# A hybrid three-mixer layer: bonus term and output gate of each token group moved from the group's own step into the next step

## The chip, the cores and the metric

The kernel runs on one core of one Trainium2 chip. The metric is the device time of one execution in microseconds (us). The kernel before took 2331.53 us, the median of three runs (2328.48 to 2334.17).

## The reference, cut to what matters

The kernel computes one layer of a token model: 1024 latent tokens and 256 context tokens, 1024 channels, one input projection, three parallel token mixers (a gated linear recurrence, an RWKV-7 mixer, an S5 state-space mixer), a gated sum with an output projection, and a SwiGLU network. The change touches the RWKV-7 mixer alone. Its width is 512, in 8 heads of 64 channels. Cut to the lines at stake (`d` is the direction):

```python
kk = heads(k * k_k); kk = kk * lax.rsqrt(jnp.sum(kk * kk, axis=-1, keepdims=True) + 1e-12)
for d in range(2):
    iclr = jax.nn.sigmoid(a0[d] + ad[:, :, d] @ a2[d])
    k_d = heads(k * (1.0 + (iclr - 1.0) * k_a))
    y_d, s_d = wkv7_scan(r_h, heads(decay), k_d, v_h, kk, heads(iclr), s0[d], d == 1)
    bonuses.append(jnp.sum(r_h * k_d * r_k, axis=-1, keepdims=True) * v_h)
y = ((y - mean) * lax.rsqrt(var + RWKV_GN_EPS)).reshape(b, l, wdt) * ln_w + ln_b
y = y + (bonuses[0] + bonuses[1]).reshape(b, l, wdt)
return y * (jax.nn.sigmoid(gd) @ g2), jnp.stack(fins)
```

The bonus term and the output gate `g = sigmoid(gd) @ g2` need nothing of the scan. The kernel prepares from them two arrays per latent token, `ln_w * g` and `(bonus + ln_b) * g`, and the scan's result is later multiplied by the first and added to the second.

## The kernel before, in words

The program is written with a framework that tracks which instruction reads and writes which tile. It puts the semaphores in by itself, and it orders the instructions of each engine by a planner: the planner runs the program against its own model of times, and among the instructions that it takes to be ready it picks the one that was written first. So the order in the source is a priority and not the order of issue. On the chip each engine then works its list off in that fixed order.

The RWKV stage prepares heads in four pairs (`p` = 0 to 3). Two heads of 64 channels fill the 128 partitions. For each pair, `rwkv_pair` (L727) loads small weights, projects and shifts the key, value and receptance, and then goes through ten groups of 128 tokens (`g` = 0 and 1 are context, 2 to 9 are latent) in a loop of eleven steps (L868). A step works on three groups at once:

- `pre(g+1)` (L765): loads two low-rank inputs (`wdt`, L768, on SyncE), eight matmuls (L774), a tanh (`swa`, L777), and on VectorE a rescale (L778) and two scans along time (`cum`, L780 and L781).
- `mid(g)` (L785): two exponentials on ScalarE (`pf`, `pi`, L797 and L798), products on GpSimd (`t`, L807 and L809; `pcend`, L799 and L800) and on VectorE (`kr`, L810 and L814; `kb`, L811 and L812). For a latent group it then forms the bonus and the gate: a sum `ks` on GpSimd (L818), a product `ks` on VectorE (L819), two matmuls into one PSUM bank (L821: the sum over a head's channels; L822: `g2`), two VectorE instructions (`vs`, L824; `glt`, L825), one on ScalarE (`glt`, L826) and one store by SyncE (`gld`, L827).
- `fill(seg_fill)` (L875): two, two, one or four pieces (by pair) of an independent projection for the branch gates (`zg`, L1333; matmuls at L1309, three to a piece).
- `post(g-1)` (L830): 32 small matmuls of `kb` with `kr` (L843), four transposes (L855), one masked copy on VectorE (`al`, L844), five copies on ScalarE (`aq`, L851; `kt`, L856), five stores by SyncE (L857, L865).

The projections of the head pair's own inputs are the matmuls at L1303, which the planner lets run among the steps. After the eleven steps, a triangular inverse per pair (L895) starts on VectorE (L901, L904, L905) and goes on as some 60 small products on GpSimd (pairs 0 to 2) or VectorE (pair 3 and the context's own inverse; `nt`, L909 and L911). The next pair's preparation starts beside it; the reciprocal `rn` (L748) belongs to that.

In pair 3 step 9 drains the filler, and step 10 starts the scan over 40 chunks (`rwkv_chain`, L920), which runs for the next several hundred us. Its first dependent step needs the context's inverse.

What the tiles allow: matmul results go through five PSUM banks of one tag (`aux`, L1857), used in turn by `pre`, `mid` and `post`. The tiles `ks` and `vs` have two buffers each, `glt` has one. A write into a tile waits until the readers of its older content in that buffer are done.

Of the kernel before, what the change touches and what calls it, by code (L numbers as in the profile page):

```python
# [9 lines left out]
F32 = mybir.dt.float32  # L10
F32R = mybir.dt.float32r
AF = mybir.ActivationFunctionType
ALU = mybir.AluOpType
# [3 lines left out]
P = 128  # L17
# [618 lines left out]
class RwkvMixin:  # L636
# [90 lines left out]
    def rwkv_pair(s, p, pool):  # L727
        nc = s.nc
        V, G, S = nc.vector, nc.gpsimd, nc.scalar
        segs = ((0, NCTX), (NCTX, 512), (NCTX + 512, 512))  # L730
        c1 = lambda key: s.pv(key)[:, p : p + 1]
# [5 lines left out]
        g2 = pool.tile([P, P], F32, name="g2", tag="g2")  # L737
        nc.sync.dma_start(g2, s.i["rwkv_g2"][0][:, cols])
        k = s.rk_next or s.shift(12 + p, True, pool, "zk", 2)
# [4 lines left out]
        for t0, n in segs:  # L744
            ps = s.aux()
# [5 lines left out]
        st = {}  # L751
# [33 lines left out]
        def mid(g):  # L785
            lat = g > 1
            sl = slice(P * g, P * g + P)
            gl0 = P * (g - 2)
# [24 lines left out]
            if lat:  # L813
                V.tensor_tensor(kr[:, :, :, 32:64], bc(st["r"]), pcur, op=ALU.mult)  # L814
                ks = pool.tile([P, P], F32, name="ks", tag="ks", bufs=2)
                vs = pool.tile([P, P], F32, name="vs", tag="vs", bufs=2)
                k2 = t2.rearrange("p d c t -> p d (c t)")
                G.tensor_tensor(ks, k2[:, 0], k2[:, 1], op=ALU.add)  # L818
                V.scalar_tensor_tensor(ks, st["r"][:, sl], c1("rk"), ks, op0=ALU.mult, op1=ALU.mult)  # L819
                ps = s.aux()  # L820
                nc.tensor.matmul(ps[:, 0:P], s.bones, ks, start=True, stop=True)  # L821
                nc.tensor.matmul(ps[:, P : 2 * P], g2, s.gdt[:, gl0 : gl0 + P], start=True, stop=True)  # L822
                glt = pool.tile([P, 2, P], F32, name="glt", tag="glt")
                V.tensor_tensor(vs, ps[:, 0:P], st["v"][:, sl], op=ALU.mult)  # L824
                V.scalar_tensor_tensor(glt[:, 1], vs, c1("lnb"), ps[:, P : 2 * P], op0=ALU.add, op1=ALU.mult)  # L825
                S.activation(glt[:, 0], ps[:, P : 2 * P], AF.Copy, scale=c1("lnw"))  # L826
                nc.sync.dma_start(s.gl_d.rearrange("a k c t -> c a k t")[:, p, :, gl0 : gl0 + P], glt)  # L827
            st[g] = [kb, kr]

        def post(g):  # L830
            lat = g > 1
# [36 lines left out]
        for g in range(11):  # L868
            if g < 9:
                pre(g + 1)  # L870
            if g < 10:
                mid(g)
            if g == RSEG:
                vr()
            s.fill(s.seg_fill)  # L875
            if g:
                post(g - 1)
            if p == 3 and g == 2:
                s.rwkv_ctx_inverse(pool)
            if p == 3 and g == CB:  # L880
                s.chain_begin()
            if p == 3 and g in CTX_AT:
                next(s.chain)
            if p < 3 and g == 7:
                s.rk_next = s.shift(13 + p, True, pool, "zk", 2)
# [1096 lines left out]
```

## Time and profile before

| what | value |
|---|---|
| median of the runs | 2331.53 us |
| the profiled execution's own time | 2331.55 us |
| its span, first to last instruction | 2329.8 us |
| granted TensorE clock over the span | 0.952 of full |
| TensorE matmul busy | 2102.5 us (90%) |
| VectorE busy | 1508.0 us (65%) |
| ScalarE busy | 904.2 us (39%) |
| GpSimd busy | 986.0 us (42%) |

In the rows, PE is TensorE (matmuls), PEld its weight loads, DVE is VectorE, ACT is ScalarE, POOL is GpSimd, SP is SyncE. L819 is line 819 of the kernel. Times count from the first instruction. An arrow with an engine behind a bracketed number says how long the engine stood idle and what ended it. One matmul of the program in 32-bit floats shows as two records. A clock of 0.50 means that TensorE was granted 1.2 GHz of its 2.4 GHz.

The latent groups of the four pairs run from 741 to 803 us, 837 to 911, 944 to 1013 and 1033 to 1120; between them lie the starts of the next pair.

### The profile page before, as it was taken

Reading aid. Unit: us, or ns where it says so; the run is one execution under the profiler, and the core shown is the slowest. Engines: PE = TensorE matmul, PEld = TensorE weight load, DVE = VectorE, ACT = ScalarE, POOL = GpSimd, SP = SyncE. Lnnn points to the kernel's source line nnn. Section 1 sums busy time; section 2 is a strip of 40 time slices with the busy share of each in tenths; the row PEclk is TensorE's granted clock in tenths of the full one; section 3 lists DMA queues with packets and bytes.
Section 4 is the critical chain, followed back from the end, with each engine's and each line's share of the span. In section 5 each row is a group of like instructions: output and inputs, shape, how many; then the busy total and the mean of one; then the engine's idle time right before and its main releaser. Section 6 shows DMA issues by size and latency. Waiting matters only on the chain.

```text
span 2329.8 us, 38390 instructions
## 1 busy us (share of the span) xinstructions
PE 2102.5 (90%) x14573; PEld 1675.7 (72%) x14573; DVE 1508.0 (65%) x2218; ACT 904.2 (39%) x1698; POOL 986.0 (42%) x1169
## 2 busy tenths in 40 slices
PE   5979988887899988898699999898999999989998
PEld 3868866665778877776467676676788888878886
DVE  5656698889566888899843366936855555543533
ACT  5313354423334645454533333416433323233431
POOL 3662389955323494856100122544644444300302
PEclk8989999998999999998699999998999999999999
DMA  6634322221663535445967777544222222274540
GB/s 254 168 110 115 90 66 83 82 84 64 143 174 89 161 111 140 125 136 142 246 181 173 171 191 183 167 158 136 81 77 86 77 86 77 68 276 151 165 149 36
DMA packets 360550, 307.26 MB, mean 132 GB/s; under 512 B 66023, under 2 KB 311982, under 8 KB 359342
## 3 DMA queue, kind: packets, MB, share of 16 engines
q1 hardware_dynamic: 356782, 293.27, 43.5%
q10 hardware_dynamic: 2880, 10.49, 1.2%
q8 instruction: 115, 1.88, 0.3%
q0 software_dynamic: 704, 1.05, 0.2%
q14 instruction: 69, 0.57, 0.1%
HBM read 219.03 MB, written 85.70 MB: 131 GB/s over the span
## 4 chain that ended last, share of the span: by engine, by line
PE 56%; DVE 19%; POOL 9%; DMA 7%; issue 5%; ACT 3%; SPq 1%; DVEq 0%; POOLq 0%; ACTq 0%
PE mm L1563 18%; PE mm L1718 10%; PE mm L1303 8%; PE mm L1309 7%; PE cg L1011 2%; PE cg L985 2%; PE cu L998 2%; DMA wm<-in_w_mod_dram 1%; DVE zl L1296 1%; PE cy L1026 1%; POOL s L214 1%; DVE s5ct L522 1%; PE aux L609 1%; DVE macc L1269 1%; DVE rn L748 1%
## 5 line engine op out<-in xcount | busy, mean ns | idle before, releaser
L1563 PE MATMUL mm<-q,wt 128*128 128x512 f32 x1584 | 376.6, 398 | 4.5 <-DVE q L1477 3.2
L1563 PEld LDWEIGHTS mm<-q,wt 128*128 128x128 f32 x1584 | 299.4, 189 | 77.5 <-DVE q L1477 3.6
L1718 PE MATMUL mm<-wk,hk 128*128 128x512 f32 x960 | 224.2, 396 | 0.0
L1303 PE MATMUL mm<-xh,wh 128*128 128x512 f32 (+1 forms) x576 | 214.4, 380 | 8.4 <-ACT ya L180 6.1
L1303 PE MATMUL mm<-xl,wh 128*128 128x512 f32 (+1 forms) x576 | 214.3, 379 | 1.2 <-DVE xl L1219 1.2
L1718 PEld LDWEIGHTS mm<-wk,hk 128*128 128x128 f32 x960 | 180.4, 188 | 43.6
L1309 PE MATMUL mm<-xh,zh 128*128 128x512 f32 x384 | 159.6, 416 | 10.0 <-ACT zge L1345 5.8
L1309 PE MATMUL mm<-xl,zh 128*128 128x512 f32 x384 | 159.5, 415 | 0.0
L1303 PE MATMUL mm<-xh,wl 128*128 128x512 f32 (+1 forms) x576 | 141.2, 383 | 8.8 <-DVE wl L1296 6.6
L1303 PEld LDWEIGHTS mm<-xh,wh 128*128 128x128 f32 x576 | 114.3, 199 | 28.6 <-ACT ya L180 6.9
L1671 DVE TENSOR_TENSOR wk<-wraw,wk 128x512 fp32r<-128x512 f32 x80 | 55.9, 707 | 111.3 <-ACT wk L1670 111.3
L1303 PEld LDWEIGHTS mm<-xl,wh 128*128 128x128 f32 x576 | 113.8, 197 | 19.4 <-DVE xl L1219 1.5
L1309 PE MATMUL mm<-byt,bwh 128*128 128x512 f32 x384 | 118.6, 428 | 7.9 <-ACT bwh L1295 2.9
L1303 PEld LDWEIGHTS mm<-xh,wl 128*128 128x128 f32 x576 | 102.9, 197 | 30.1 <-DVE wl L1296 8.2
L1309 PE MATMUL mm<-xh,zl 128*128 128x512 f32 x384 | 110.1, 423 | 15.3 <-DVE zl L1296 15.3
L1691 POOL TENSOR_TENSOR acc<-acc,ot 128x512 f32<-128x512 f32 x14 | 19.0, 1358 | 225.7 <-DVE ot L1689 225.2
L1015 DVE TENSOR_TENSOR x<-cg,pcend 64x256 f32<-64x256 f32 x152 | 63.9, 421 | 77.9 <-PE cg L1011 35.4
L1476 ACT ACTIVATE wt<-wT 128x512 fp32r<-128x512 f32 x88 | 55.1, 631 | 142.5 <-PE mm L1563 130.5
L1309 PEld LDWEIGHTS mm<-xh,zl 128*128 128x128 f32 x384 | 75.4, 202 | 35.2 <-DVE zl L1296 18.3
L1269 DVE SCALAR_TENSOR_TENSOR macc<-wm,cs,macc 128x256 f32<-128x256 f32 x112 | 84.6, 755 | 22.3 <-DMA wm<-in_w_mod_dram 19.8
L1477 DVE TENSOR_TENSOR wt<-wt 128x512 fp32r<-128x512 f32 x66 | 60.5, 918 | 59.4 <-ACT wt L1476 59.0
L1293 POOL CAST bwh<-bwr 128x512 fp32r<-128x512 f32 x16 | 10.0, 624 | 209.6 <-PE mm L1309 112.1
(421 smaller groups left out, 4865.3 us busy)
## 6 DMA issues: line engine op xcount, KB each, us to landing
wt<-in_w_ffn_in_dram SPq DMA_DIRECT2D x44, 512.0 KB
wraw<-in_w_ffn_out_dram SPq DMA_DIRECT2D x44, 512.0 KB
wm<-in_w_mod_dram SPq DMA_DIRECT2D x64, 256.0 KB
gyl<-gyl SPq DMA_DIRECT2D x32, 512.0 KB
wr<-in_w_in_dram SPq DMA_DIRECT2D x27, 512.0 KB
zr<-in_w_in_dram SPq DMA_DIRECT2D x24, 512.0 KB
sgd<-zge SPq DMA_DIRECT2D x48, 256.0 KB
bsg<-sgd SPq DMA_DIRECT2D x48, 256.0 KB
```

Source lines behind the costliest of these rows:

```text
L985: s.pe = nc.tensor.matmul(ps[32 * q : 32 * q + 32, 64 * p : 64 * p + 64], gy[:, 2 * p + par, c - cb, 0:32], st["x"][:, p, par, :], start=T ...
L998: s.pe = nc.tensor.matmul(ps[o : o + 32, 64 * p : 64 * p + 64], st["tt"][32 * q : 32 * q + 32, p, st["cc"], :], st["gs"][32 * q : 32 * q + ...
L1011: s.pe = nc.tensor.matmul(sn[64 * par : 64 * par + 64, 64 * p : 64 * p + 64], sd[:, st["cc"], 2 * p + par, :], st["x"][:, p, par, :], star ...
L1015: V.tensor_tensor(xn[0:64, :, par, :], sn[r].rearrange("p (a k) -> p a k", a=4), vb(s.pcend[r, d, :, st["c"]], 64), op=ALU.mult)
L1269: nc.vector.scalar_tensor_tensor(acc, wm[:, j], s.cs[:, k + j, 0:1], acc, op0=ALU.mult, op1=ALU.add)
L1303: s.nc.tensor.matmul(ps, w(k), a(k), start=n == 0, stop=n == len(seq) - 1)
L1309: s.nc.tensor.matmul(ps, w[:, k], a[:, k], start=n == 0, stop=n == len(seq) - 1)
L1476: s.nc.scalar.activation(hi, raw, AF.Copy)
L1477: (eng or s.nc.vector).tensor_tensor(lo, raw, hi, op=ALU.subtract)
L1563: nc.tensor.matmul(ps, w[:, k], a[:, k], start=n == 0, stop=n == len(seq) - 1)
L1671: V.tensor_tensor(hl[:, 1], raw, hl[:, 0], op=ALU.subtract)
L1718: nc.tensor.matmul(banks[t, n], a[:, tk], b, start=k == 0 and q == 0, stop=k == NF - 1 and q == 2)
```

## The change: what it does

The part of `mid(g)` that begins with the two matmuls becomes a function of its own, `gate(g)`. The sum and the product that make `ks` stay in `mid(g)`; the tile is kept until the gate is formed. In the loop, `gate(g-1)` is written behind `post(g-1)`, so the gate of group `g` moves from the middle of step `g` to the end of step `g+1`. The instructions themselves, their shapes and buffers are as before.

```diff
             if lat:
                 V.tensor_tensor(kr[:, :, :, 32:64], bc(st["r"]), pcur, op=ALU.mult)
                 ks = pool.tile([P, P], F32, name="ks", tag="ks", bufs=2)
-                vs = pool.tile([P, P], F32, name="vs", tag="vs", bufs=2)
                 k2 = t2.rearrange("p d c t -> p d (c t)")
                 G.tensor_tensor(ks, k2[:, 0], k2[:, 1], op=ALU.add)
                 V.scalar_tensor_tensor(ks, st["r"][:, sl], c1("rk"), ks, op0=ALU.mult, op1=ALU.mult)
-                ps = s.aux()
-                nc.tensor.matmul(ps[:, 0:P], s.bones, ks, start=True, stop=True)
-                nc.tensor.matmul(ps[:, P : 2 * P], g2, s.gdt[:, gl0 : gl0 + P], start=True, stop=True)
-                glt = pool.tile([P, 2, P], F32, name="glt", tag="glt")
-                V.tensor_tensor(vs, ps[:, 0:P], st["v"][:, sl], op=ALU.mult)
-                V.scalar_tensor_tensor(glt[:, 1], vs, c1("lnb"), ps[:, P : 2 * P], op0=ALU.add, op1=ALU.mult)
-                S.activation(glt[:, 0], ps[:, P : 2 * P], AF.Copy, scale=c1("lnw"))
-                nc.sync.dma_start(s.gl_d.rearrange("a k c t -> c a k t")[:, p, :, gl0 : gl0 + P], glt)
+                st["ks", g] = ks
             st[g] = [kb, kr]
+
+        def gate(g):
+
+            sl = slice(P * g, P * g + P)
+            gl0 = P * (g - 2)
+            ks = st.pop(("ks", g))
+            vs = pool.tile([P, P], F32, name="vs", tag="vs", bufs=2)
+            ps = s.aux()
+            nc.tensor.matmul(ps[:, 0:P], s.bones, ks, start=True, stop=True)
+            nc.tensor.matmul(ps[:, P : 2 * P], g2, s.gdt[:, gl0 : gl0 + P], start=True, stop=True)
+            glt = pool.tile([P, 2, P], F32, name="glt", tag="glt")
+            V.tensor_tensor(vs, ps[:, 0:P], st["v"][:, sl], op=ALU.mult)
+            V.scalar_tensor_tensor(glt[:, 1], vs, c1("lnb"), ps[:, P : 2 * P], op0=ALU.add, op1=ALU.mult)
+            S.activation(glt[:, 0], ps[:, P : 2 * P], AF.Copy, scale=c1("lnw"))
+            nc.sync.dma_start(s.gl_d.rearrange("a k c t -> c a k t")[:, p, :, gl0 : gl0 + P], glt)
@@
             s.fill(s.seg_fill)
             if g:
                 post(g - 1)
+            if g > 2:
+                gate(g - 1)
             if p == 3 and g == 2:
                 s.rwkv_ctx_inverse(pool)
```

## Rows read from the trace of the kernel before

**Rows 1.** Busy time in stretches: length, then each engine's busy us (instructions), clock, DMA.
```profile
741.00:803.00 62.00, 57.37 (x594) 50.45 (x593) 49.70 (x100) 39.24 (x96) 28.74 (x49) 0.94 0.65 179
837.00:911.00 74.00, 64.11 (x600) 54.86 (x599) 56.98 (x99) 39.40 (x93) 47.52 (x84) 0.92 0.56 154
944.00:1013.00 69.00, 64.26 (x617) 56.01 (x617) 54.66 (x97) 40.60 (x96) 48.73 (x90) 0.95 0.54 149
...
1033.00:1120.00 87.00, 68.82 (x592) 56.90 (x591) 82.58 (x160) 39.16 (x96) 59.23 (x95) 0.88 0.55 148
```

**Rows 2.** Who waited for whom, TensorE, 741 to 1033: us, times, longest.
```profile
PE aux L821 <- DVE ks L819: 11.9, 6, 3.1
```

**Rows 3.** The same view for 1033 to 1120.
```profile
PE aux L821 <- DVE ks L819: 6.3, 3, 4.3
```

**Rows 4.** Timeline of TensorE around four waits: start, us, instruction, [idle before <- releaser].
```profile
756.45 0.59 PE L821 MATMUL aux<-ks,bones 128*128 128x128 f32 x2 [1.14 <-DVE ks L819]
...
797.44 0.62 PE L821 MATMUL aux<-ks,bones 128*128 128x128 f32 x2 [2.27 <-DVE ks L819]
...
798.42 1.97 PE L843 MATMUL aux<-kr,kb 64*64 64x64 f32 x32
...
905.30 0.49 PE L821 MATMUL aux<-ks,bones 128*128 128x128 f32 x2 [3.00 <-DVE ks L819]
...
957.85 0.60 PE L821 MATMUL aux<-ks,bones 128*128 128x128 f32 x2 [3.09 <-DVE ks L819]
```

**Rows 5.** Busy time in stretches at half clock, with their sum; columns as in Rows 1.
```profile
756.60:760.00 3.40, 3.40 (x40) 3.06 (x40) 2.16 (x7) 2.62 (x7) 0.00 (x0) 0.51 0.37 122
...
958.00:964.80 6.80, 6.80 (x52) 6.22 (x53) 4.26 (x10) 3.61 (x10) 6.57 (x13) 0.50 0.25 61
sum 20.40, PE 20.40 PEld 18.07 DVE 14.09 ACT 15.45 POOL 9.65; mean PE 4.08 PEld 3.61 DVE 2.82 ACT 3.09 POOL 1.93
```

**Rows 6.** The chain that ended last, 797 to 811: start, us, what.
```profile
797.03 0.27 DVE ks L819
...
797.44 0.62 PE aux L821 x2
...
801.29 1.08 PE aux L843 x32
...
805.09 1.24 DVE aq L901
```

**Rows 7.** Timeline of the two sides of the `ks` buffers, GpSimd and TensorE.
```profile
768.42 0.45 POOL L818 TENSOR_TENSOR ks<-t 128x128 f32<-128x128 f32 x1
...
974.48 0.45 POOL L818 TENSOR_TENSOR ks<-t 128x128 f32<-128x128 f32 x1
...
1113.68 0.60 POOL L818 TENSOR_TENSOR ks<-t 128x128 f32<-128x128 f32 x1
...
767.78 0.66 PE L855 MATMUL aux<-ident,kb 128*128 128x128 f32 x4
...
974.11 0.38 PE L821 MATMUL aux<-ks,bones 128*128 128x128 f32 x2
...
975.72 0.66 PE L855 MATMUL aux<-ident,kb 128*128 128x128 f32 x4
...
1113.78 1.11 PE L855 MATMUL aux<-ident,kb 128*128 128x128 f32 x4
```

**Rows 8.** Groups by line, 741 to 1120: busy us, mean ns, idle before, releasers.
```profile
L819 DVE SCALAR_TENSOR_TENSOR ks<-zr,pv,ks 128x128 f32<-128x128 f32 x32 | 15.9, 498 | 19.2 <-POOL ks L818 18.9 <-POOL gst L1074 0.3
L825 DVE SCALAR_TENSOR_TENSOR glt<-vs,pv,aux 128x128 f32<-128x128 f32 x31 | 10.6, 343 | 4.4 <-DMA gld<-glt 3.1 <-ACT kk L743 0.9
L824 DVE TENSOR_TENSOR vs<-aux,zr 128x128 f32<-128x128 f32 x32 | 8.9, 279 | 3.9 <-PE aux L822 3.9
L826 ACT ACTIVATE glt<-aux,pv 128x128 f32<-128x128 f32 x31 | 11.2, 361 | 36.2 <-issue 21.5 <-DVE glt L825 14.7
```

**Rows 9.** Who waited for whom, SyncE's queue, 741 to 1140.
```profile
SPq L827 <- ACT glt L826: 50.2, 18, 5.4
```

## The prediction

> **What bounds the kernel now.** The change lives in the four pairs of heads, 741 to 1120 us, so I read first the table of busy time for the latent groups of each pair [rows 1]. In pairs 0 to 2 TensorE is busy 57.37 of 62 us, 64.11 of 74 and 64.26 of 69, and VectorE 49.70, 56.98 and 54.66: TensorE is the fuller one, at 87 to 93%, and neither is full. What is missing there is lost to waits between engines. In pair 3 it is the other way round: VectorE is busy 82.58 of 87 us and TensorE 68.82, because two inverses run on VectorE. Second, the view of who waited for whom. In the first 292 us TensorE's largest wait is for `ks` (L819), which its bonus matmul L821 needs: 11.9 us in 6 waits [rows 2]. In pair 3 it is 6.3 us in 3 [rows 3]. Third, the timeline at four of these waits: 1.14, 2.27, 3.00 and 3.09 us [rows 4]. The reader is to see that what stands behind the waiting L821 is `post` of the group before (L843 at 798.42), whose inputs are older than `ks`. So TensorE stands in front of work that it could do.
>
> Fourth, the granted clock. Behind each of these four waits TensorE ran at 0.50 or 0.51, that is 1.2 GHz: 3.4 us from 756.6, 797.6 and 906.8, and 6.8 us from 958.0. One more such stretch, of 3.4 us, makes the sum of five 20.40 us, and TensorE was busy in all of it [rows 5]. Fifth, the chain that ended last: at the end of pair 0 it goes from `ks` at 797.03 through L821 and `post` of group 9 (801.29) to the start of the inverse on VectorE at 805.09 [rows 6]. There the wait and the slow clock both lie on the path.
>
> **The change part by part.** Nothing is removed or added: each of the 32 latent groups has the same two matmuls, two VectorE instructions, one ScalarE instruction and one store. They go behind `post` of the same group, one step later.
>
> *TensorE's wait.* In the new place `ks` is a step old. The four waits come to 1.14 + 2.27 + 3.00 + 3.09 = 9.5 us, and the half clock behind them (17.0 of the 20.4 us) to 8.5 us of lost matmul time, since TensorE was busy throughout: 18.0 us together. What of it lies on the path: the two waits at the ends of pairs 0 and 1 (797.44 and 905.30) hold up the last two `post`, and the first of them is in the chain as a whole [rows 6]. I count both in full: 2.27 + 1.7 + 3.00 + 1.7 = 8.7 us. The other two (756.45 and 957.85) cost 1.14 + 1.7 + 3.09 + 3.4 = 9.3 us. There TensorE, once free, soon comes to work whose inputs VectorE makes, and VectorE is itself busy for 79 to 80% of those pairs [rows 1]. Late next is `kb`, which VectorE writes shortly before `ks`. I take half, 4.6 us. Gain: 13.3 us. Bounds: nothing, if each wait is taken over by the next; and 11.9 us plus half of 20.4, that is 22.1, if all come back.
>
> *Pair 3.* VectorE has 4.4 us free in 87 [rows 1], so TensorE's 6.3 us [rows 3] are hidden beside it: nothing. Bounds: 4.4 us gained; 2 us lost, if the last gate's 0.28 + 0.34 us on VectorE [rows 8] and the waits around them end up at the close of the stage.
>
> *The wait that the change adds.* `ks` has two buffers. GpSimd's L818 of group g+2 writes into the one that L821 of group g reads. Before, L821 had read it a step earlier. Now it stands behind the transposes of `post(g)`, and takes 0.38 us [rows 7]. I set, for all 24 groups that have a group two later in their pair, the end of L855 plus 0.38 us against the start of L818 two groups on. In 16 the buffer is free in time. In 8 it is not: the first is 768.44 + 0.38 - 768.42 = 0.40 us, the largest 976.38 + 0.38 - 974.48 = 2.28, the last 1114.89 + 0.38 - 1113.68 = 1.59 [rows 7]; all eight come to 8.5 us. Queued behind L818 on GpSimd are the products of the inverse, and VectorE's L819 waits for it, which already stood 18.9 us for GpSimd in 32 groups [rows 8]; behind L819 stand the products of the next group. Part of this is taken back when TensorE, free of its own wait, reaches `post` earlier. I take six tenths, 5.1 us lost. Bounds: 0 and 8.5.
>
> *ScalarE, VectorE and SyncE.* ScalarE sits idle 36.2 us before its copy L826, 14.7 of them until VectorE's L825, and VectorE 3.9 us before `vs` and 3.1 us before `glt` for the earlier store [rows 8]; SyncE stands 50.2 us for L826 in 18 waits [rows 9]. The block moves as a whole, so the distances inside it stay: I count nothing. It now stands behind `post`'s copies and five stores, which no longer queue behind it, and in front of the next step's tanh and `wdt` load. Bounds: 7.0 us gained, if VectorE's two waits go; 5.4 us lost, the longest of SyncE's waits, if one lands before a load that TensorE needs.
>
> The two matmuls share one PSUM bank, which VectorE and ScalarE both read. The Trainium skill, PSUM — Partial Sum Buffer, section "PSUM bank collisions raise a hardware error", says that these two engines must not access one bank on the same 32 partitions at once, two reads included. By that rule ScalarE's 14.7 us follow the gate wherever it stands, as counted; without it up to 14.7 us of ScalarE's idle time would be free to go, though ScalarE bounds no pair.
>
> Sum: 13.3 gained, 5.1 lost, 8.2 us net. Against the profiled execution's own 2331.55 us (the median of the runs is 2331.53, so no correction) this gives 2323.3; I say 2323 us.
>
> **The rivals.**
>
> *The wait changes its owner.* TensorE no longer waits for `ks` but for `kb`, which lies just ahead of `ks` in VectorE's order, and the stretches at half clock stay. For it: in each pair VectorE is busy for three quarters of the time or more [rows 1]. Against it: at the pair ends the work behind the wait is `post` of an older group. Time: 13.3 shrinks to about 5, and the 5.1 lost eat it: 2331.5, give or take 3.
>
> *The two `ks` buffers decide.* This is the slower side. Place: GpSimd's L818. Price: if TensorE gets nothing back and the eight waits reach VectorE in full, 2331.5 + 8.5 = 2340. For it: in a third of the groups GpSimd already comes too early, and GpSimd is what VectorE waited for most [rows 8]. Against it: the planner knows of the buffer and can put products of the inverse ahead of L818. It decides from the point at which these waits exceed what TensorE gets back.
>
> *The planner does not do what the source says.* The source gives priorities; the planner may have TensorE take the gate early, when it thinks TensorE has nothing else, and a wait for `ks` remains. For it: the order on each engine is the planner's. Against it: filler is mostly at hand. Time: 2331.5.
>
> *All comes back*: 22.1 and VectorE's 7.0 us together would be 2302.4; I price the middle between this and the forecast, 2312.
>
> **How the numbers follow.** A measurement of this kernel tells about 0.2% from no change, 4.7 us. Chances: the forecast 0.51, the larger gain 0.06, the changed owner 0.17, the planner 0.06, the buffers 0.20. Faster by over 0.2%: 0.57; within: 0.23; slower: 0.20. For the forecast alone 2314 to 2327. The range, 2309 to 2340, reaches up to the price of the buffers and down past the larger gain, and leaves out some 2 in 10.
>
> **What would show it.** Right: TensorE's waits for `ks` fall from 18.2 us to under 3; fewer than 10 us at half clock in pairs 0 to 2, against 20.4; the inverse of pair 0 starts some 4 us sooner. Wrong: GpSimd's L818 with waits for the gate's matmul, or VectorE's wait for L818 well above 18.9 us; TensorE waiting as long before L843 as it did before L821. The planner's rival shows as L821 still ahead of `post` of its group on TensorE. The forecast fails altogether if a moved store holds up the loads behind it on SyncE, or the scan's start comes no earlier although the pairs are shorter.

## The result: 0.5% slower, and the profile after

The changed kernel takes 2342.8 us (median of five runs, 2339.1 to 2349.1) against 2331.5 us. The ratio is 1.0051, with a 95% interval of 1.0036 to 1.0067, so some 11 us slower: above the forecast range (2309 to 2340), and slower where a gain was forecast. The profiled execution has a span of 2337.4 us, 7.6 us above that of before. Lines of `gate` and behind it have new numbers: the sum `ks` is L817 (GpSimd) and L818 (VectorE), the gate's matmuls are L829 and L830, `vs` L832, `glt` L833 (VectorE) and L834 (ScalarE), its store L835; lines from 828 on have moved by nine.

The order that the planner gave each engine is the same in both kernels up to the latent groups of pair 0, and again from some 50 us into the scan, but for one swap near 1312 us. So each execution can be cut at the same instructions:

| us | before | changed |
|---|---|---|
| program start to the latent groups of pair 0 | 741.7 | 738.8 |
| to the end of the context's inverse (four pairs) | 389.1 | 389.4 |
| to the scan's first dependent step | 8.6 | 14.0 |
| first eight chunks of the scan | 61.3 | 64.1 |
| rest of the scan | 253.9 | 252.1 |
| end of the scan to the end of the program | 875.3 | 879.0 |

The first row has the same order of instructions in both, and so shows how far two executions differ by themselves (734 to 745 us over all the executions below). The other rows add up to 10.4 us lost. The four pairs, on which the whole prediction was built, come out even. What was lost lies behind them: 5.4 us before the scan's first dependent step, 2.8 in its first eight chunks, 3.7 behind the scan, less 1.8 in the rest of the scan. Each column is one execution, that of the changed kernel the fastest of its five.

Busy time of the changed kernel in the latent groups of the four pairs, then in the start of pair 3, columns as in [rows 1]:

```profile
738.80:803.20 64.40, 60.83 (x614) 52.82 (x613) 51.81 (x101) 43.08 (x103) 28.44 (x50) 0.97 0.70 191
833.60:909.80 76.20, 68.85 (x633) 58.02 (x633) 58.02 (x101) 43.07 (x105) 47.10 (x81) 0.94 0.59 164
940.70:1015.10 74.40, 64.02 (x614) 54.44 (x613) 60.19 (x102) 42.86 (x104) 48.29 (x82) 0.95 0.62 166
1039.80:1115.90 76.10, 65.05 (x580) 52.58 (x579) 68.96 (x142) 37.08 (x93) 48.38 (x83) 0.90 0.55 151
1015.10:1039.80 24.70, 22.50 (x107) 18.44 (x106) 24.66 (x19) 9.00 (x16) 20.97 (x33) 0.95 0.05 14
```

The start of pair 3 before, in the same view:

```profile
1020.00:1033.50 13.50, 12.44 (x67) 10.36 (x66) 13.42 (x5) 6.83 (x9) 7.19 (x17) 1.00 0.27 77
```

Cut at the same instructions, the latent groups of pairs 0 to 3 went from 66.7, 80.5, 75.4 and 86.5 us to 64.5, 76.3, 74.4 and 76.0. But the starts of pairs 1, 2 and 3 went from 29.0, 26.8 and 13.6 us to 30.3, 30.9 and 24.7. Up to the end of pair 2's groups that leaves a gain of 2.0 us; it is gone at the end of the inverse. VectorE was busy for 93 and 96% of the starts of pairs 1 and 2 before, and for 91 and 89% after. In pair 3's start it is busy throughout in both kernels (24.66 of 24.70 us, 13.42 of 13.50): its work has moved from the groups into the start, and sits there in TensorE's way.

Who waited for whom in the changed kernel, TensorE, 738 to 1116 (us, times, longest):

```profile
PE aux L760 <- DVE zr L705: 10.7, 3, 4.5
PE aux L829 <- ACT aq L858: 5.7, 6, 2.1
...
PE aux L829 <- ACT kt L863: 3.0, 2, 1.9
```

The waits for `ks`, 11.9 and 6.3 us [rows 2, 3], have fallen to one of 0.7. In their place TensorE waits for ScalarE's copies before the gate (L829), and 10.7 us for VectorE at the starts of the pairs (L760). VectorE's own waits, 741 to 1131 of the kernel before:

```profile
DVE ks L819 <- POOL ks L818: 18.9, 12, 3.2
DVE swa L778 <- ACT swa L777: 6.7, 10, 0.9
...
DVE zp L703 <- POOL zr L702: 3.1, 2, 1.7
DVE glt L825 <- DMA gld<-glt: 3.1, 3, 1.4
...
DVE kr L810 <- ACT pf L797: 1.5, 1, 1.5
```

and 738 to 1128 of the changed one:

```profile
DVE glt L833 <- DMA gld<-glt: 11.9, 7, 5.1
DVE swa L778 <- ACT swa L777: 10.4, 9, 5.0
DVE zp L703 <- POOL zr L702: 9.6, 3, 3.8
DVE kr L810 <- ACT pf L797: 6.9, 9, 2.2
...
DVE ks L818 <- POOL ks L817: 0.8, 2, 0.4
```

VectorE's wait for GpSimd's `ks` went too (18.9 to 0.8 us), which the prediction had not counted. Others grew by nearly as much: its idle time up to the end of the context's inverse is 56.0 us before and 60.1 after. The groups by line that answer to [rows 8], 738 to 1116:

```profile
L818 DVE SCALAR_TENSOR_TENSOR ks<-zr,pv,ks 128x128 f32<-128x128 f32 x32 | 14.0, 438 | 0.9 <-POOL ks L817 0.8
...
L817 POOL TENSOR_TENSOR ks<-t 128x128 f32<-128x128 f32 x32 | 18.2, 569 | 0.5
...
L834 ACT ACTIVATE glt<-aux,pv 128x128 f32<-128x128 f32 x31 | 11.3, 365 | 29.4 <-DVE glt L833 21.3 <-issue 7.9
```

and SyncE's wait that answers to [rows 9], 738 to 1140:

```profile
SPq L835 <- ACT glt L834: 23.8, 18, 4.9
```

Behind the pairs. SyncE's queue at the start of the scan, before (the context's inverse ends at 1130.7; `gl` is what the scan loads of the gates, `tt` its inverses, `ttd` the store that `tt` needs, `byr` operands of the branches):

```profile
1131.38 0.37 SPq L1363 DMA_DIRECT2D byr<-yd  x1
1131.85 0.55 SPq L893 DMA_DIRECT2D ttd<-aqc  x1
...
1133.12 1.21 SPq L1083 DMA_DIRECT2D gl<-gld  x1
...
1136.26 2.54 SPq L949 DMA_DIRECT2D tt<-ttd  x4
```

and in the changed kernel, where that inverse ends at 1128.2:

```profile
1126.36 2.02 SPq L1372 DMA_DIRECT2D byr<-yd  x2
...
1130.17 0.38 SPq L835 DMA_DIRECT2D gld<-glt  x1
1131.77 0.57 SPq L902 DMA_DIRECT2D ttd<-aqc  x1
1132.73 2.76 SPq L1092 DMA_DIRECT2D gl<-gld  x4
1135.59 1.18 SPq L1372 DMA_DIRECT2D byr<-yd  x2
1136.86 2.52 SPq L958 DMA_DIRECT2D tt<-ttd  x4
```

`ttd` goes out 3.6 us after the inverse has ended, in place of 1.1. The last gate of pair 3 is now done later (ScalarE's copy ends 2.4 us ahead of the inverse's end, 7.5 us in the kernel before), and its store (1130.17) stands ahead of `ttd`; behind it SyncE waits at `ttd` until an older load has landed (`gyc`, another operand of the scan):

```profile
SPq L902 <- DMA gyc<-gyc: 1.2, 1, 1.2
```

`tt` reads what `ttd` has stored, so it can't go out before `ttd` has landed. In the kernel before that took 4.4 us and set the time of `tt`, as the chain that ended last shows:

```profile
1131.85 4.35 DMA ttd<-aqc
...
1136.26 2.92 DMA tt<-ttd
```

By its semaphore events `ttd` took 4.4 us in the changed kernel too, to 1136.2. So the four `gl` loads (three of which had gone out before the inverse's end in the kernel before) and the two `byr` loads that now stand between `ttd` and `tt` hold `tt` up by some 0.7 us only. `tt` goes out 8.7 us after the inverse instead of 5.5. From there to the scan's first dependent step it was 3.1 us before and 5.3 after: those loads are still under way beside `tt`. While `tt` travels the DMA engines are busier than before (columns as in [rows 1]; the last two numbers are their busy share, whose count can run a little over 1, and GB/s). Before:

```profile
1136.26:1139.18 2.92, 0.00 (x0) 0.00 (x0) 2.71 (x10) 0.13 (x1) 0.00 (x0) 0.50 0.56 141
```

and after:

```profile
1136.86:1142.02 5.16, 0.00 (x0) 0.00 (x0) 4.38 (x13) 0.86 (x2) 0.00 (x0) 0.50 1.03 278
```

So of the 5.4 us 2.5 are the later `ttd`, some 0.7 the loads ahead of `tt`, and 2.2 the slower `tt`. TensorE at the scan's first dependent step, before:

```profile
1139.32 1.06 PE L998 MATMUL mm<-gs,tt 32*32 32x64 f32 x16 [5.20 <-DMA tt<-ttd]
```

and after:

```profile
1142.16 1.06 PE L1007 MATMUL mm<-gs,tt 32*32 32x64 f32 x16 [14.94 <-DMA tt<-ttd]
```

The last place is 380 us further on, where the branch sums (`bsg`) end and the output product begins (L1303, now L1312). Every engine stands in the same order there. VectorE and TensorE before:

```profile
1516.61 0.67 DVE L1376 SCALAR_TENSOR_TENSOR bsg<-bsg,mm 128x512 f32<-128x512 f32 x1
...
1517.34 2.98 PE L1303 MATMUL mm<-wt,q 128*128 128x512 f32 x7 [2.27 <-DVE bsg L1376]
...
1519.47 0.69 DVE L1376 SCALAR_TENSOR_TENSOR bsg<-bsg,mm 128x512 f32<-128x512 f32 x1 [1.59 <-DMA bsg<-sgd]
```

and after:

```profile
1519.22 0.68 DVE L1385 SCALAR_TENSOR_TENSOR bsg<-bsg,mm 128x512 f32<-128x512 f32 x1
...
1522.09 0.69 DVE L1385 SCALAR_TENSOR_TENSOR bsg<-bsg,mm 128x512 f32<-128x512 f32 x1 [1.60 <-DMA bsg<-sgd]
...
1522.83 1.65 PE L1312 MATMUL mm<-wt,q 128*128 128x512 f32 x3 [5.16 <-DVE bsg L1385]
```

Before, the output's first product waits for the last branch sum but one (1516.61 + 0.67 = 1517.28); after, for the last (1522.09 + 0.69 = 1522.78). The wait is 5.16 us instead of 2.27. The clock falls to half for 10.2 us instead of 3.4; in the changed kernel it falls while TensorE still waits (at 1518.8), and 6.2 us of it lie behind the wait. The stretch of half clock before, columns as in [rows 1]:

```profile
1517.80:1521.20 3.40, 3.40 (x10) 2.61 (x9) 1.37 (x3) 0.63 (x1) 2.11 (x2) 0.50 0.90 295
```

and after:

```profile
1518.80:1529.00 10.20, 6.17 (x15) 4.81 (x16) 3.67 (x6) 3.01 (x6) 3.60 (x3) 0.50 0.70 218
```

Why the product waits for another sum is a matter of PSUM banks. The branch sums use three banks in turn (0, 1, 2), and when they are through, the output stage takes all eight; its first product gets bank 0. In the built programs bank 0 was held by the last sum but one before, and by the last sum after: the change shifted the turn.

### The profile page after: what moved, and what is told of

The parts are those of the page before. It is cut to its first block, busy times and chain, and to the rows that moved or that the text cites. A ratio compares the mean times of both kernels' runs of the same rounds, so it can differ in the third digit from the quotient of the medians.

```text
span 2337.4 us, 38412 instructions
## 1 busy us (share of the span) xinstructions
PE 2104.6 (90%) x14573; PEld 1675.8 (72%) x14573; DVE 1505.9 (64%) x2218; ACT 905.0 (39%) x1698; POOL 994.7 (43%) x1169
## 4 chain that ended last, share of the span: by engine, by line
PE 44%; DVE 3%; DMA 2%; issue 2%; ACT 1%; POOL 1%; SPq 0%; DVEq 0%; POOLq 0%; ACTq 0%
PE mm L1572 18%; PE mm L1727 10%; PE mm L1318 5%; PE mm L1312 3%; PE cg L1020 3%; PE cg L994 2%; PE cu L1007 2%; DMA byr<-yd 1%; PE cy L1035 1%; DVE q L1416 0%; DVE bwl L1305 0%; DVE bsg L1385 0%; DVE q L1486 0%; DVE wt L1486 0%; DMA bsg<-sgd 0%
## 5 line engine op out<-in xcount | busy, mean ns | idle before, releaser
L1312 PE MATMUL mm<-xh,wh 128*128 128x512 f32 (+1 forms) x576 | 216.7, 383 | 6.7 <-ACT ya L180 4.5
L1312 PE MATMUL mm<-xl,wh 128*128 128x512 f32 (+1 forms) x576 | 215.4, 381 | 1.2 <-DVE xl L1228 1.2
L1318 PE MATMUL mm<-xh,zh 128*128 128x512 f32 x384 | 164.2, 428 | 10.7 <-ACT zge L1354 5.8
L1312 PE MATMUL mm<-xh,wl 128*128 128x512 f32 (+1 forms) x576 | 136.8, 376 | 6.1 <-DVE wl L1305 5.0
L1312 PEld LDWEIGHTS mm<-xh,wh 128*128 128x128 f32 x576 | 114.9, 200 | 27.3 <-ACT ya L180 5.4
L1312 PEld LDWEIGHTS mm<-xl,wh 128*128 128x128 f32 x576 | 114.7, 199 | 19.4 <-DVE xl L1228 1.4
L1312 PEld LDWEIGHTS mm<-xh,wl 128*128 128x128 f32 x576 | 101.2, 192 | 26.1 <-DVE wl L1305 6.2
L1278 DVE SCALAR_TENSOR_TENSOR macc<-wm,cs,macc 128x256 f32<-128x256 f32 x112 | 85.1, 760 | 24.7 <-DMA wm<-in_w_mod_dram 22.6
L1318 PEld LDWEIGHTS mm<-xh,zh 128*128 128x128 f32 x384 | 77.0, 200 | 31.3 <-ACT zge L1354 6.2
```

The costliest lines, as they stand in the source:

```text
L1278: nc.vector.scalar_tensor_tensor(acc, wm[:, j], s.cs[:, k + j, 0:1], acc, op0=ALU.mult, op1=ALU.add)
L1312: s.nc.tensor.matmul(ps, w(k), a(k), start=n == 0, stop=n == len(seq) - 1)
L1318: s.nc.tensor.matmul(ps, w[:, k], a[:, k], start=n == 0, stop=n == len(seq) - 1)
```

## The experiments

Ratios are to the kernel before, measured beside each on the same chip, with 95% intervals. "Behind the inverse" is the time from the end of the context's inverse to the scan's first dependent step (8.6 us before, 14.0 after), "the tail" that from the end of the scan to the end of the program (875.3 and 879.0).

### The start of the scan, and which pairs matter

The first theory (Q) was that `byr` loads in SyncE's queue are the loss, since the chain of waits of the changed kernel runs through three of them:

```profile
1126.36 7.37 DMA byr<-yd
...
1136.39 5.38 DMA byr<-yd
1141.79 5.00 DMA byr<-yd
```

Its rivals were the one `glt` buffer (B) and the late last gate of pair 3 (P). Two kernels put these loads behind the first `tt` loads, two others move the gate in some pairs only.

g_after (changed) and g_before (before):
```diff
-            s.y0 = s.branch_y(s.ya_d, 0)
+            with s.tc.issue_after(s.sp.ins):   # s.sp: the newest tt load
+                s.y0 = s.branch_y(s.ya_d, 0)
```


> The changed kernel, with the eight loads of the first branch's input (byr, at the end of pair 3) tied behind the scan's first tt loads on SyncE's queue. Theory Q (the loss is at the start of the scan: in the changed kernel's plan the byr loads stand on SyncE ahead of the context inverse's store, and ScalarE and VectorE cast byr in front of the scan's own copies): the first dependent step of the scan (cu) starts by about 1135 us instead of 1142, and the time falls by 6 to 11 us, to 2332 to 2337 us. Theory B (the pairs themselves got slower, by the single glt buffer, for which VectorE waits 11.9 us): nothing changes in the pairs, so the time stays at 2340 to 2345.

> The kernel before with the same tie: byr loads behind the first tt loads. Theory Q: its byr loads were early already (first at 1117 us), so it gains little: 2327 to 2332 us, and beside it the changed kernel with the tie shows what the move itself does to the pairs: a gain of 2 to 5 us. Theory B: 2329 to 2333 us, and the changed kernel with the tie stays 8 to 12 us behind it.

Measured: 2338.9 us, 1.0039 (1.0025 to 1.0053), and 2331.1 us, 1.0010 (0.9999 to 1.0021). Behind the inverse it is still 14.1 us in g_after: two `gl` loads and the last gate's store now stand ahead of `ttd`, which goes out 6.3 us after the inverse, and takes 5.3 us to land. Q falls as a whole explanation.

a_p012 (gate moved in pairs 0 to 2) and b_p3 (in pair 3 alone):
```diff
                 st["ks", g] = ks
+                if not (p < 3):      # b_p3: p == 3
+                    gate(g)
...
-            if g > 2:
+            if g > 2 and (p < 3):
                 gate(g - 1)
```


> The gate moved in pairs 0 to 2 alone; in pair 3 it stays in its own step. Theory Q: the plan at the start of the scan is dealt anew here too, and byr again stands ahead of the store of the context's inverse: slower than before, 2336 to 2345 us. Rival P (the last gate of pair 3, behind its post, is what delays the scan): no loss, 2326 to 2332 us. Theory B: two thirds of the loss, 2336 to 2340 us, with VectorE's wait for the glt store still about 8 us.

> The gate moved in pair 3 alone. In this plan byr comes behind the first tt loads. Theory Q: not slower than before, 2325 to 2332 us. Rival P: the whole loss, 2338 to 2345 us. Theory B: a quarter of the loss, 2333 to 2336 us.

Measured: 2337.8 us, 1.0034 (1.0022 to 1.0045), and 2336.0 us, 1.0028 (1.0018 to 1.0039). Either part alone is slower; the two together (0.51%, 0.36 to 0.67) lose no more than their sum, 0.62%. a_p012 has 7.4 us behind the inverse, like the kernel before, but its inverse ends 5.3 us later and the wait at the output product is 5.34 us. b_p3 has 12.5 us behind the inverse and the wait of 2.27 us as before. So the late start of the scan belongs to pair 3 (theory P), and the pairs gain nothing in either. It isn't the last gate's store by itself: in b_p3 `ttd` goes out at once, ahead of that store and of every `gl` load; other loads of the scan stand between it and `tt`, which takes 6.0 us to land.

### Waits inside the pairs

Each of these asks one theory: c_glt2 whether it is the single `glt` buffer (C), h_gldpool whether it is the last gate's store in SyncE's queue (S; pair 3's stores go to GpSimd's), n_gatefirst and m_after_aux6 whether it is the PSUM tiles for which the gate waits (M). L is the theory that any new order costs something.
```diff
-            glt = pool.tile([P, 2, P], F32, name="glt", tag="glt")
+            glt = pool.tile([P, 2, P], F32, name="glt", tag="glt", bufs=2)      # c_glt2
```
```diff
-            nc.sync.dma_start(s.gl_d.rearrange("a k c t -> c a k t")[:, p, :, gl0 : gl0 + P], glt)
+            (G if p == 3 else nc.sync).dma_start(s.gl_d.rearrange("a k c t -> c a k t")[:, p, :, gl0 : gl0 + P], glt)
```
```diff
+            if g > 2:                # n_gatefirst
+                gate(g - 1)
             if g:
                 post(g - 1)
-            if g > 2:
-                gate(g - 1)
```
```diff
-        s.mmp = op("mmp", bufs=3, space=PSUM)
-        s.auxp = op("auxp", bufs=5, space=PSUM)
+        s.mmp = op("mmp", bufs=2, space=PSUM)      # m_after_aux6
+        s.auxp = op("auxp", bufs=6, space=PSUM)
```


> The changed kernel with two glt buffers in place of one, so that a gate's cast need not wait for the store of the gate before. Theory C (the single glt buffer is what makes VectorE lose the time that it gained: it waits 11.9 us for that store in the four pairs): the wait for the store goes, the context inverse ends about 6 to 10 us sooner and the time is 2332 to 2336. Theory S (the wait is one of several that stand in for one another, and the end of the last gate is what costs): the wait goes, other waits of VectorE grow by as much, and the time is 2337 to 2343. Theory L (any new order that the planner deals costs a few microseconds): 2336 to 2345 with the projections spread anew over the pairs.

> The changed kernel with the eight gate stores of pair 3 issued by GpSimd instead of SyncE, so that none stands in SyncE's queue ahead of the store of the context inverse and of the scan's first loads. Theory S (the last gate's store holds up SyncE at the start of the scan): from the end of the context inverse to the first dependent step of the scan 14.0 us become about 8.5, and the time is 2335 to 2338. Theory C: the single glt buffer is still there, VectorE's waits stay, the time is 2340 to 2344. Theory L: no term of its own, 2336 to 2345.

> The changed kernel with the gate of the group before put ahead of post of that group instead of behind it. The gate's PSUM tile is then taken after the same tiles as in the kernel before (pre, gate, post), and its store goes ahead of post's five. Theory M (the gate waits for a PSUM tile that post's copies hold, 10.7 us of TensorE's waits for aq, kt and swa): these waits fall below 4 us and the time is 2331 to 2335. Theory S: the last gate is done before post, its store is out of the way earlier, and the wait before the scan shrinks to about 9 us: 2335 to 2338. Theory C: VectorE still waits for the glt store, 2339 to 2343. If the wait for ks comes back, TensorE's waits for it are above 3 us.

> The changed kernel with six PSUM tiles instead of five in the ring from which the gate and post take theirs, and two instead of three in the ring of the projections. Theory M (PSUM tiles): TensorE's waits for aq, kt and swa at the gate go, the pairs shorten by 5 to 8 us, and the time is 2332 to 2337, unless the projections lose by their smaller ring (in which case pairs 0 to 2 get longer). Theory C or S: 2338 to 2345.

Measured: 2337.8 us, 1.0037 (1.0023 to 1.0052); 2349.3 us, 1.0076 (1.0064 to 1.0088); 2347.9 us, 1.0072 (1.0060 to 1.0085); 2342.8 us, 1.0053 (1.0040 to 1.0066). In c_glt2 VectorE's wait for the gate's store falls to 1.6 us, and the inverse ends 384.7 us after the start of pair 0's groups in place of 389.4. But 16.8 us follow behind the inverse, and the scan starts only 1.9 us earlier. Part of the expectation of C held (the pairs), the time did not. h_gldpool has no gate store ahead of `ttd`, which goes out 1.3 us behind the inverse; but it takes 6.4 us to land, with `byr` and `gl` loads beside it, another `byr` load goes out ahead of `tt`, and `tt` takes 5.5 us: 14.4 us in all. S named the wrong member of the queue. Why this kernel is the slowest of all is open. In n_gatefirst and m_after_aux6 the waits shift again (in n_gatefirst TensorE waits 6.7 us for `ks`) and the inverse ends 393.2 and 395.7 us after the start. Neither bears M out, but m_after_aux6 doesn't refute it: TensorE's waits at the gate halve, to 5.4 us, while the projections, left with two tiles, wait 8.2 us for ScalarE, and pairs 0 to 2 get 6.6 us longer, which is the exception that M had named. All four have 13 to 17 us behind the inverse.

### The loads in front of `tt`

r_gl ties the `gl` loads behind the scan's first `tt` loads, r_by the `byr` loads too, r_2 adds two `glt` buffers; r_before is the kernel before with both ties.
```diff
         for k in range(2):
-            nc.sync.dma_start(gl[:, k], s.gl_d.rearrange("a k c t -> k c a t")[k, :, :, P * b : P * b + P])
+            with s.tc.issue_after(s.sp.ins):   # s.sp: the last of the first four tt loads
+                nc.sync.dma_start(gl[:, k], s.gl_d.rearrange("a k c t -> k c a t")[k, :, :, P * b : P * b + P])
```


> The changed kernel with the scan's loads of gl (they wait for the last gate's store) tied behind the scan's first four loads of tt on SyncE. Theory S (moving pair 3's gate puts the gl loads and the last gate store between the store of the context inverse and the tt loads, and the scan starts later): from the end of the context inverse to the first dependent step of the scan 14.0 us become 8 to 11, and the time is 2335 to 2340. If VectorE's end of the context inverse is what costs (theory V): the stretch shortens but the time stays 2340 to 2345.

> The changed kernel with both the gl loads and the first byr loads tied behind the first tt loads; only the store of the last gate can still stand ahead of them. Theory S: 14.0 us become about 7 to 9, as in the kernel before and its variant with the byr loads tied (8.6 and 6.7), and the time is 2332 to 2337, what stays being the first eight chunks of the scan, 3 to 6 us longer when byr lands among them. Theory V: 2338 to 2345.

> The same with two glt buffers, in whose plan the context inverse ended 4.4 us sooner after the start of pair 0 (384.7 us in place of 389.1). If both add up, the first dependent step comes 392 to 394 us after the start of pair 0's latent groups, against 397.6 in the kernel before, and the time is 2326 to 2332. If they do not add up, because the new order is dealt anew: 2333 to 2342.

> The kernel before with the same two ties (gl and byr loads behind the first tt loads). Theory S: the stretch there is short already, so it is worth 0 to 3 us: 2328 to 2333. A loss over 3 us would mean that the ties themselves cost time, and would have to be added to what r_by shows.

Measured: r_gl 2334.4 us, 1.0021 (1.0010 to 1.0032); r_by 2338.1 us, 1.0043 (1.0028 to 1.0057); r_2 2337.2 us, 1.0033 (1.0021 to 1.0045); r_before 2324.2 us, 0.9985 (0.9970 to 0.9999). Behind the inverse the four have 12.3, 8.8, 13.3 and 6.0 us. r_gl was faster than expected with a longer place than expected; its profiled execution was its slowest (2339.9 us), so its cuts say little, and why it beats r_by is open. In r_2 the two gains don't add up. In r_by `ttd` goes out 1.3 us behind the inverse with the gate's store still ahead of it, and though nothing stands between, SyncE waits 4.4 us for it to land before `tt`:

```profile
SPq L959 <- DMA ttd<-aqc: 4.4, 1, 4.4
```

The step follows `tt` by 2.5 us (5.3 in the changed kernel). In r_by the place is as short as in the kernel before (8.6 us), and 0.43% are still lost, so the start of the scan is not the whole loss. The tail tells why: 878.5 us in r_by, 870.1 in r_before. At the output product TensorE waits 5.13 us in r_by and not at all in r_before, where bank 0 was last held by the last sum but two. That turn of the banks, more than the tie's own place, is also what makes r_before faster than the kernel before: 0.9 us less in the pairs, 2.6 less behind the inverse, 5.6 more in the first eight chunks, 5.2 less in the tail.

### The bank of the output's first product

s_after and s_before left three tiles of the output stage's pool unused (theory T: it is the bank); t_after and t_before have the ties besides.
```diff
         s.mmp = op("mm2", bufs=8, space=PSUM)
+        for _ in range(3):
+            s.mm()
```


> The changed kernel with three PSUM tiles of the output stage's pool left unused at its opening, so that its first products go to banks that the last branch sums don't hold; the order of every engine is that of the changed kernel. Theory T (part of the loss sits far behind the pairs: the first product of the output stage lands in the bank of the last branch sum, so TensorE waits 5.2 us instead of 2.3 and runs 10.2 us instead of 3.4 at half clock): no gap over 1 us there, end of the scan to the end of the kernel 879 us becomes 870 to 874, and the time falls by 5 to 9 us, to 2333 to 2338. If that stretch is bound by something else (the loads of the output weights): the gap goes, the stretch stays above 877, 2340 to 2344.

> The kernel before with the same three tiles left unused, its order unchanged. Theory T: its wait there is 2.3 us and its half clock 3.4 us, so the gain is smaller, 3 to 5 us: 2325 to 2328, and the difference between the kernels shrinks from 11 to 7 us or less. Without theory T: 2329 to 2332.

> The changed kernel with both repairs: gl and byr loads tied behind the scan's first tt loads, and the three tiles left unused. If start of scan and output stage hold the whole loss (theories S and T): 2326 to 2331, that is the kernel before. What stays above its twin without the change (t_before) is what the pairs and the first chunks of the scan cost.

> The kernel before with both repairs. Its tied version alone ran at 2324.2 and had no wait at the output stage already, so the tiles are worth nothing to it: 2321 to 2326. With S and T as the whole loss t_after and t_before differ by less than 3 us; if they differ by 5 us or more, the pairs themselves cost time.

Measured: s_after 2347.2 us, 1.0068 (1.0055 to 1.0081); s_before 2333.0 us, 1.0000 (0.9989 to 1.0012); t_after 2344.1 us, 1.0053 (1.0040 to 1.0065); t_before 2328.3 us, 0.9987 (0.9976 to 0.9997). All four came out above the time expected with theory T. The first two say nothing of it: a tile that nothing writes gets no bank, and the first product still sat in bank 0 (its waits are 5.97 and 2.27 us). The engines stand in the order of the changed kernel, of the kernel before, of r_by and of r_before, and so show how well a ratio repeats: 1.0051 and 1.0068 (changed), 1.0000 (before), 1.0043 and 1.0053, 0.9985 and 0.9987. They show it for the cuts too: behind the inverse 14.0 and 16.8 us (changed), 8.6 and 8.2 (before), 8.8 and 11.1, 6.0 and 5.9; the tail 879.0 and 881.3, 875.3 and 876.9, 878.5 and 881.2, 870.1 and 870.8. So a single difference of cuts is good to some 3 us.

u_after takes the three banks of the branch sums from the other end of PSUM (5 to 7), so that nobody holds bank 0; u_rby adds the ties of r_by.
```diff
-        s.mmp = op("mmp", bufs=3, space=PSUM)
+        s.mmp = op("mmp", bufs=3, space=PSUM, **R)      # R: side="right"
```


> The changed kernel with the three PSUM banks of mmp taken from the other end of PSUM (banks 5 to 7 instead of 0 to 2), so that bank 0, into which the output stage's first product goes, is not held by a branch sum; in the built program that product then carries no wait, and the order of TensorE is the same up to it. (The unused tiles of s_after got no bank at all, and its first product waited as before.) Theory T: no gap over 1 us at the output stage, end of the scan to the end of the kernel 870 to 873 us in place of 879, and the time is 2333 to 2338. Without theory T: the gap goes and the stretch stays above 877, 2340 to 2345.

> The same with the gl and byr loads tied behind the scan's first tt loads. Its twin without the change is r_before (and t_before, whose engines stand in the same order), which has the tie and no wait at the output stage: 2324.2 and 2328.3. If start of scan and output stage are the whole loss: 2323 to 2329. If the pairs and the first chunks of the scan cost time of their own: 2330 to 2335, with the stretch from the pairs to the end of the context inverse 1 to 3 us longer than in r_before.

Measured: u_after 2335.6 us, 1.0017 (1.0008 to 1.0026); u_rby 2330.3 us, 1.0005 (0.9992 to 1.0017). As theory T has it; but u_rby's time, and its stretch to the inverse (1.4 us longer than in r_before), are what was expected if the pairs and the first chunks cost time of their own. TensorE at the output product of u_after:

```profile
1520.72 1.19 PE L1318 MATMUL mm<-byt,bwl 128*128 128x512 f32 x4 [0.72 <-DVE bwl L1305]
1521.75 7.63 PE L1312 MATMUL mm<-wt,q 128*128 128x512 f32 x32
```

No wait, and full clock behind it:

```profile
1521.75:1556.00 34.25, 34.25 (x148) 27.63 (x147) 13.43 (x18) 7.36 (x12) 15.80 (x11) 1.00 0.58 207
```

The tail is 870.7 us in u_after and 869.2 in u_rby. In u_rby SyncE's queue has nothing left between `ttd` and `tt`:

```profile
1127.79 0.38 SPq L835 DMA_DIRECT2D gld<-glt  x1
1128.26 0.57 SPq L903 DMA_DIRECT2D ttd<-aqc  x1
1132.99 2.52 SPq L959 DMA_DIRECT2D tt<-ttd  x4
```

and the DMA engines have room while `tt` travels (share and GB/s are the last two numbers, against 1.03 and 278 in the changed kernel):

```profile
1132.99:1135.30 2.31, 0.00 (x0) 0.00 (x0) 2.10 (x7) 0.00 (x0) 0.00 (x0) 0.50 0.17 40
```

The same cuts as above, for the kernels that settle it:

| us | r_by | u_after | u_rby | r_before |
|---|---|---|---|---|
| to the latent groups of pair 0 | 739.8 | 739.3 | 737.2 | 734.1 |
| to the end of the context's inverse | 389.4 | 389.5 | 389.6 | 388.2 |
| behind the inverse | 8.8 | 15.5 | 8.6 | 6.0 |
| first eight chunks | 63.9 | 63.8 | 68.9 | 66.9 |
| rest of the scan | 254.2 | 253.6 | 250.6 | 253.5 |
| tail | 878.5 | 870.7 | 869.2 | 870.1 |

What each place is worth. The bank: from the changed kernel to u_after the ratio falls by 0.34%, from r_by to u_rby by 0.38%, some 8 us. That is more than its part in the loss, because the kernel before pays for its own wait of 2.27 us too: its tail is 875.3, and 870.1 in r_before, which has none. By the cuts the bank's part in the loss is 3.7 us (4.4 between s_after and s_before). The start of the scan: 5.4 us behind the inverse, and the ties take it back (14.0 to 8.8 us, 15.5 to 8.6). In the ratio they are worth less than that between these pairs, 0.08 and 0.12%, which is not clear of the noise; in the second pair the first chunks get longer (63.8 to 68.9 us), where the `byr` loads then fall. The 2.8 us of the first eight chunks stay unexplained. With both repairs the changed kernel runs like the kernel before. Against the kernel before with the same ties and without a wait at the output product (r_before and t_before) it still loses 0.2%, some 4 us. That rest is not settled: against r_before the cuts give 3.1 us ahead of the pairs, where the order is the same, 1.4 in the pairs, 2.6 behind the inverse and 2.0 in the first chunks, and 3.8 are taken back behind them. Theory L, that a new order costs by itself, has no more than this left. The version that beats both kernels is r_before, without the change, by 0.15%.

## Why the prediction was wrong

**The wait that was to go did go.** TensorE's waits for `ks` fell to 0.7 us ("under 3" was asked), L829 stands behind `post` of its group, and the inverse of pair 0 starts at 799.4 instead of 805.1, 2.7 us sooner after the start of the pair's groups ("some 4").

**Its size in the sum failed: 13.3 us gained were 0.** This is the first failed step: 2.0 us were left at the end of pair 2's groups, and none at the end of the inverse. The sum counted the waits at the pair ends in full, because there they were in the chain that ended last. But what follows a pair is the next pair's start, and VectorE was busy there for 93, 96 and 99% of the time already. The four groups' stretches became 18 us shorter together, and the three starts 16.5 longer. That VectorE is what ate the gain is read from these busy times and from TensorE's wait for `zr`; no run tests it by itself. The lower bound that the prediction gave itself, "nothing, if each wait is taken over by the next", was the value. Its changed-owner rival described the pairs rightly, with the owner wrong: not `kb` but `zr` at the starts (10.7 us) and ScalarE's copies ahead of the gate. The half clock did not fall either: 27.2 us up to pair 3's groups before (the 20.4 of [rows 5] and two more stretches), 30.7 after, 13.7 of them from the end of a wait for `zr` (4.0 us) at the start of pair 1 on.

**The `ks` buffers cost nothing, not 5.1 us.** GpSimd's L817 stood idle 0.5 us in all, and VectorE's wait for it, which [rows 8] has at 18.9 us, went nearly to nothing. The overlap of starts was read from the order of before; in the planner's new order L817 of group g+2 starts 0.4 us or more behind L829 of group g, in every group. The slower rival built on this had the right side and nearly the right time, 2340, by luck: its mechanism did not occur.

**The moved block is not free: "I count nothing" failed.** This is the second failed step. VectorE waited 11.9 us for the store of the one `glt` buffer instead of 3.1. The store doesn't queue longer (it goes out 0.3 us behind ScalarE's copy on average in both kernels); why it is then waited for longer is open. And with pair 3's gate moved the scan's start came 5.4 us later, by a late `ttd` and by `gl` and `byr` loads beside `tt`. The bound of that step named the case ("if one lands before a load that TensorE needs"); that its price of 5.4 us, the longest of SyncE's waits in [rows 9], is also what was measured is luck. The last sentence named the case again as the way in which "the forecast fails altogether". It was given no chance of its own, though the code shows which loads need the last gate. ScalarE's copy went with the gate as counted: it stood 21.3 us behind VectorE's L833 (14.7 before, [rows 8]). That agrees with the Trainium skill, PSUM — Partial Sum Buffer, section "PSUM bank collisions raise a hardware error", by which the two engines must not read one bank on the same partitions at once. The copy was not quite without cost: in the pairs TensorE waited 5.1 us for it, 3.5 before.

**One term was in no list.** 3.7 us come from a PSUM bank 380 us behind the last changed instruction. The prediction took it for granted that a stage whose order does not change keeps its time.

## What to carry to other kernels

A wait that stands in the chain of one stage's end is worth its length only if the engine that the next stage starts with has room; add up the engine's idle time over the whole phase, to the point where something outside consumes the result. When a moved instruction ends in a store, list the loads that need that store, and see what stands behind them in their queue and what travels beside it, as the prediction did in words and should have done in numbers. And where buffers are handed out in turn, moving any work can shift whose buffer the next stage inherits: look at the first instruction of each later stage, and give it a buffer that nobody holds.

## What the runs showed of the hardware

How much a short pause of TensorE costs at the output product: around a pause of 2.3 us (with a shorter one, of 0.3 to 0.9 us, ahead of it) the granted clock was 0.50 for 3.4 us in three kernels and 6.8 in one, at 3.9 us for 3.4 us in m_after_aux6, at 5.1 to 6.1 us for 6.8 or 10.2 us in eleven, and without a pause not at all (r_before, t_before, u_after, u_rby). So 2.9 us of added wait made the tail 3.7 us longer, and taking the whole 5.2 us away made it 8.3 us shorter (879.0 to 870.7).

What other transfers cost a small one: `tt` landed 2.3 us after its issue with the DMA engines at a busy share of 0.17 (u_rby), 2.9 us at 0.56 (before), and 5.2 us at 1.03 (changed). The 256 KB `byr` loads took 5.0 to 7.4 us each in the chain at the start of the scan.
